# One step of a hybrid decoder on Trainium2: the up-projection's first block product in three passes, and another order for scale, operands and weight sums of the first pairs

## The chip, the cores and the metric

The kernel runs on one core of one Trainium2 chip. The metric is the device time of one execution in microseconds (us). Engines in the profile: PE (tensor engine, matmuls), PEld (its weight loads), DVE (vector engine), ACT (ScalarE), POOL (GpSimd), SP (the queue that issues most loads).

## What is computed

A one-layer decoder trunk is run on a prompt of 512 tokens and on 8 single-token samples, 520 columns in all. After the mixers the feed-forward part follows, on which the change works:

```python
x = x + jnp.matmul(mix, w_out)
y, conv_new = conv_ffn(rms_norm(x, norm2), w_up, conv_w, conv_b, w_down, conv_buf)

def conv_ffn(h, w_up, conv_w, conv_b, w_down, prefix):
    u = jnp.matmul(h, w_up)                       # 2048 -> 2 * 5632
    up = jnp.concatenate([prefix.astype(u.dtype), u], axis=1)
    c = conv_b
    for j in range(CONV_W):                       # causal depthwise convolution, width 3
        c = c + conv_w[j] * up[:, j:j + T]
    gate, val = jnp.split(c, 2, axis=-1)
    y = jnp.matmul(jax.nn.gelu(gate) * val, w_down)
```

Everything is float32, and the kernel must keep nearly that precision.

## The kernel before

**Products in three passes.** A float32 operand is split into hi (rounded to the reduced format fp32r, a ScalarE copy) and lo (the rest, a vector subtraction). A product is then hi x hi, hi x lo and lo x hi, three fp32r matmuls into one PSUM bank (lines 1139 to 1141, 967 and 186 to 190). A float32 matmul on unsplit operands (raw) is one instruction, which the profile shows as two records (lines 1146 and 1102).

**The up-projection in pairs.** The 88 column blocks of 128 are worked off in 44 pairs, p = 0 to 43, alternately gate and value. A pair is a 2 x 2 block product: its weights are A(p, n, i), with n the column block and i the half of the 2048 rows (even or odd blocks of 128), its operands B(i, t), with t the half of the 520 columns (260 each). From p = 1 on the pair needs seven block products instead of eight, by sums of weights and of operands. `up_units` has them as units numbered 1 to 7:

| unit | weights | operand | PSUM bank |
|---|---|---|---|
| 1 | A(p,0,0) | B11, raw | 1 |
| 2 | A(p,0,1) | B21 | 1, on top of 1 |
| 3 | S2 after `sum4` | B22 | 3, on top of 5 |
| 4 | A(p,1,1) | t4 | 4 |
| 5 | S1 | t1 | 3 |
| 6 | S2 | t2 | 2 |
| 7 | S3 | t3 | 0 |

The weight sums S1, S2 and S3 come from `sum1`, `sum2`, `sum3`, and S2 is overwritten by `sum4` (lines 1039 to 1048, vector engine, 128 x 1024 each, one buffer each). The operands t1 to t4 are sums and differences of the B(i, t); they are made once (`prep1` to `prep5`) and kept split. The results are put together by vector additions out of PSUM (`post6`, `c21`, `c22`, `post3`). Pair 0 does not use this scheme: `first_units` runs its eight products raw on xg, the activations that are not yet divided by their norm, and multiplies with that norm (rbc1) on the way out of PSUM (line 1108).

**Order of the work.** The order on each engine is that of the program. The loop at the end goes through the list of units: at unit k it first emits the split of unit k + 2 (`prod`: hi on ScalarE, lo on the vector engine, lines 929 and 931, three buffers each), then what is put ahead of unit k (`pre`: loads, weight sums, operands), then its matmuls, then `post`, then one step of each background generator. Each engine takes its instructions in this order and waits where an operand or a buffer is not ready.

**The convolution** of a finished pair (`conv`, lines 1050 to 1085) is such a generator. It begins with two small GpSimd copies and two ScalarE activations (line 1060) and goes on with four vector steps (line 1065), one per unit of the next pair. After a gate pair follows a ScalarE GELU, after a value pair a vector multiplication (line 1072) and a store.

**Loads.** `load_pair` loads the two blocks of a pair, 1 MB each, on the SP queue: block 0 into a buffer with two copies, block 1 into a single one (r2), so that the load of the next pair's block 1 waits for the lo of unit 4.

**Ahead of the up-projection** the output projection ends (line 967); `split_x2` makes for each pair of its blocks the scaled activations xg (`gain`, line 994), the squares (line 1005) and their sum (line 1007, GpSimd). `norm2` (called by `prep1`) sums the squares over the rows by matmuls with a constant (line 1223) and makes 1/rms (lines 1224 to 1226 on ScalarE, `newton` on the vector engine). `normed` multiplies xg by it (line 1233), `diff` subtracts (line 1247), `split_act` splits (lines 1241 and 1242). `prep0` stores the sums x2b to memory (GpSimd queue). Before the change these preparations hang on four units of pair 0 (one for each n and i, both halves t in it) and on two units of pair 1.

**After it** the down-projection (line 967) takes its operands back from memory (`load_a`, GpSimd queue, and `split_a`).

## Time and profile before

| | before |
|---|---|
| three runs, us | 2345.4, 2345.03, 2345.9 |
| median, us | 2345.4 |
| profiled execution, us | 2346.91 |
| its span on the core, us | 2345.0 |
| mean granted clock of the tensor engine | 0.993 |
| ScalarE busy, us | 863.0 (37%) |
| GpSimd busy, us | 185.1 (8%) |
| bytes moved | 268.68 MB, 115 GB/s |

In a row of a timeline stand the start in us from the span's start, the duration, the engine, the line of the kernel, the operation, what it writes and reads, and in brackets the idle time ahead of it with what ended that. In a row of waits stand who waited, for whom, the sum in us, how often, and the longest. In the chain of the work that ended last stand start, length and work; a number behind x counts the instructions in it. Pair 0 begins at 858.94 us of the span.

### The profile page before, as it was taken

The page shows a single profiled execution, that of the slowest core. Times are in us where ns is not written, and L with a number is a line of the kernel's source. Part 1 is how long each engine was busy: PE and PEld are TensorE (multiplying, and loading weights), DVE is VectorE, ACT ScalarE, POOL GpSimd, SP SyncE. Part 2 cuts the span into 40 slices and gives each one's busy share as a digit, 9 for nine tenths or more (in the row PEclk, how much of TensorE's full clock was granted, in tenths as well). Part 3 has the DMA queues.
Part 4 walks back from the last instruction along what each step waited for, and adds up shares of the span by engine and source line. Part 5 has one row for each costly group of instructions (what it writes and reads, how often), then busy time and mean ns, then how long its engine had stood idle before and what let it go on. Part 6 is the DMA issues. An engine that isn't in the chain of part 4 may idle for free.

```text
span 2345.0 us, 42285 instructions
## 1 busy us (share of the span) xinstructions
PE 2302.1 (98%) x18268; PEld 2260.4 (96%) x18268; DVE 1414.2 (60%) x1963; ACT 863.0 (37%) x1245; POOL 185.1 (8%) x397
## 2 busy tenths in 40 slices
PE   8999999999999997999999999999999999999996
PEld 8999999999999997999999999999999999999996
DVE  4365655445543448888878888788887433434346
ACT  6233342313342434444444444444444222222225
POOL 0001021021010120000000000000000000000002
PEclk9999999999999998999999999999999999999998
DMA  5322233334251443433334343343435523323214
GB/s 183 102 82 93 89 94 97 95 108 131 73 172 61 141 129 89 122 105 118 110 117 127 100 124 105 116 127 103 124 107 188 218 90 132 127 91 109 91 55 136
DMA packets 313353, 268.68 MB, mean 115 GB/s; under 512 B 8492, under 2 KB 299144, under 8 KB 311072
## 3 DMA queue, kind: packets, MB, share of 16 engines
q1 hardware_dynamic: 298608, 212.56, 29.5%
q0 software_dynamic: 14560, 53.43, 6.5%
q8 instruction: 144, 2.36, 0.4%
q14 instruction: 41, 0.34, 0.0%
HBM read 240.25 MB, written 28.12 MB: 114 GB/s over the span
## 4 chain that ended last, share of the span: by engine, by line
PE 73%; DVE 4%; ACT 1%; issue 1%; DMA 0%; ACTq 0%; DVEq 0%; POOLq 0%
PE pw L967 24%; PE pw L1139 10%; PE pw L1140 10%; PE pw L1141 10%; PE pw L1146 6%; PE pg L186 3%; PE pg L188 3%; PE pg L190 3%; DVE lo L931 1%; PE psc L703 1%; PE pob L685 1%; DVE n L1233 0%; PE pw L1102 0%; PE px L750 0%; ACT hi L929 0%
## 5 line engine op out<-in xcount | busy, mean ns | idle before, releaser
L929 ACT ACTIVATE hi<-r 128x1024 fp32r<-128x1024 f32 (+1 forms) x208 | 208.0, 1006 | 450.5 <-PE pw L967 364.8
L931 DVE TENSOR_TENSOR lo<-r,hi 128x1024 fp32r<-128x1024 f32 (+1 forms) x208 | 250.1, 1203 | 87.7 <-ACT hi L929 87.7
L186 PE MATMUL pg<-x1h,hi 128*128 128x260 f32 x1408 | 289.8, 287 | 3.1 <-ACT hi L157 1.8
L190 PE MATMUL pg<-x1h,lo 128*128 128x260 f32 x1408 | 284.5, 284 | 0.5 <-DVE lo L159 0.5
L188 PE MATMUL pg<-x1l,hi 128*128 128x260 f32 x1408 | 283.5, 283 | 0.0
L931 DVE TENSOR_TENSOR lo<-s,hi 128x1024 fp32r<-128x1024 f32 x172 | 210.4, 1223 | 65.3 <-ACT hi L929 65.3
L1326 DVE TENSOR_TENSOR x<-pw,x 128x260 f32<-128x260 f32 (+2 forms) x192 | 74.0, 423 | 268.3 <-PE pw L967 264.8
L159 DVE TENSOR_TENSOR lo<-raw,hi 128x1024 fp32r<-128x1024 f32 x104 | 127.2, 1223 | 168.0 <-ACT hi L157 156.4
L186 PEld LDWEIGHTS pg<-x1h,hi 128*128 128x128 f32 x1408 | 217.7, 189 | 4.4 <-ACT hi L157 2.0
L929 ACT ACTIVATE hi<-s 128x1024 fp32r<-128x1024 f32 x172 | 181.8, 1058 | 105.3 <-PE pw L1140 98.1
L190 PEld LDWEIGHTS pg<-x1h,lo 128*128 128x128 f32 x1408 | 217.5, 189 | 0.7 <-DVE lo L159 0.7
L188 PEld LDWEIGHTS pg<-x1l,hi 128*128 128x128 f32 x1408 | 217.2, 189 | 0.0
L1065 DVE SCALAR_TENSOR_TENSOR cv<-u,convc,cv 128x512 f32<-128x512 f32 (+1 forms) x176 | 132.2, 751 | 43.8 <-ACT cv L1060 43.8
L1146 PE MATMUL pw<-n,r 128*128 128x260 f32 x688 | 157.7, 382 | 0.0
L1146 PEld LDWEIGHTS pw<-n,r 128*128 128x128 f32 x688 | 127.6, 190 | 17.7
L157 ACT ACTIVATE hi<-raw 128x1024 fp32r<-128x1024 f32 x104 | 109.6, 1056 | 43.5 <-PE pg L188 36.6
L1139 PE MATMUL pw<-t4h,hi 128*128 128x260 f32 x344 | 106.3, 309 | 0.0
L1139 PE MATMUL pw<-t1h,hi 128*128 128x260 f32 x344 | 98.7, 287 | 6.7 <-DVE u L1108 6.7
L1060 ACT ACTIVATE cv<-u,convc 128x512 f32<-128x512 f32 x88 | 66.8, 806 | 99.3 <-DVE u L1185 93.8
L1141 PE MATMUL pw<-b21h,lo 128*128 128x260 f32 x344 | 98.2, 285 | 2.6 <-DVE lo L931 2.6
L1141 PE MATMUL pw<-t4h,lo 128*128 128x260 f32 x344 | 98.0, 285 | 2.3 <-DVE lo L931 2.3
L1139 PE MATMUL pw<-b22h,hi 128*128 128x260 f32 x344 | 97.6, 284 | 1.1 <-DVE u L1164 1.1
(475 smaller groups left out, 6173.4 us busy)
## 6 DMA issues: line engine op xcount, KB each, us to landing
r<-in_w_up SPq DMA_DIRECT2D x88, 1024.0 KB, 5.3
raw<-in_w_in SPq DMA_DIRECT2D x88, 512.0 KB, 3.6
r<-in_w_down SPq DMA_DIRECT2D x40, 1024.0 KB, 5.1
ad<-cv POOLq DMA_DIRECT2D x22, 520.0 KB, 3.1
a<-ad POOLq DMA_DIRECT2D x11, 1040.0 KB, 5.5
raw<-in_w_out SPq DMA_DIRECT2D x16, 512.0 KB, 3.4
r<-in_w_out SPq DMA_DIRECT2D x8, 1024.0 KB, 5.2
r<-in_w_down SPq DMA_DIRECT2D x13, 512.0 KB, 3.3
```

The lines of the kernel that those rows point to most:

```text
L159: V.tensor_tensor(lo, raw, hi.bitcast(F32), op=ALU.subtract)
L186: PE.matmul(ps[:, i, 0:b - a], wh, xh[:, a:b], start=first, stop=False)
L188: PE.matmul(ps[:, i, 0:b - a], wh, xl[:, a:b], start=False, stop=False)
L190: PE.matmul(ps[:, i, 0:b - a], wl, xh[:, a:b], start=False, stop=last)
L929: S.activation(hi, view, AF.Copy)
L931: V.tensor_tensor(lo, view, hi.bitcast(F32), op=ALU.subtract)
L967: PE.matmul(ps[t][:, 0:b - a], wt[:, kk], x[:, a:b], start=kk == 0 and wt is hi and x is xh, stop=kk == nk - 1 and wt is lo)
L1065: V.scalar_tensor_tensor(cv[:, j, 0:w], u[:, j, i:i + w], convc[:, i, n], cv[:, j, 0:w], op0=ALU.mult, op1=ALU.add)
L1139: PE.matmul(ps(k), hi[:, m], xh[:, m], start=a, stop=False, skip_group_check=True)
L1140: PE.matmul(ps(k), hi[:, m], xl[:, m], start=False, stop=False, skip_group_check=True)
L1141: PE.matmul(ps(k), lo[:, m], xh[:, m], start=False, stop=z, skip_group_check=True)
L1146: PE.matmul(ps(1), A(p, 0, 0)[:, m], xop["b11"][:, m], start=m == 0, stop=m == 7, skip_group_check=True)
```

## The change

Five things are done:

- From pair 3 on unit 1 is in three passes as well: its weights A(p,0,0) are split like the others, and B11 is split once (`prep_b11`, ahead of the sixth unit of pair 2; it borrows two buffers of the convolution). In pairs 1 and 2 unit 1 stays raw. In pair 1 units 2 and 3 become raw too.
- The order of the units from pair 2 on is 1, 4, 5, 6, 7, 2, 3 instead of 1, 4, 6, 7, 5, 2, 3. The result that needs unit 5 (`c22`) is now made right after unit 7, ahead of `c21`. Pair 1 keeps 1, 5, 6, 7, 2, 4, 3.
- Pair 0 has eight units of one raw product each instead of four of two. The norm and t1 hang on the second of them, t2 on the fifth, the weight sums S1 and S2 of pair 1 on the sixth; t3 and S3 on the first unit of pair 1, B21 and t4 on its third; the splits of B21 and B22 on the last unit of pair 1 and the first of pair 2.
- For the last two blocks of the output projection only one of four gains stands ahead of the squares, and the last sum of squares is the vector engine's.
- The down-projection's operands and the last output tiles use other buffers, and the first two of these operands are both loaded on the second unit of the last pair.

```diff
@@ -988,13 +988,14 @@
 
         m = n0 // 2
 
-        def gain():
-            for i in range(2):
-                for t in range(2):
-                    S.activation(xg[i][t][:, m], x2b[i][t][:, m], AF.Copy, scale=gv[:, G2 + n0 + i:G2 + n0 + i + 1])
-
-        if n0 == KT - 2:
-            gain()
+        end = n0 == KT - 2
+
+        def gain(some):
+            for i, t in some:
+                S.activation(xg[i][t][:, m], x2b[i][t][:, m], AF.Copy, scale=gv[:, G2 + n0 + i:G2 + n0 + i + 1])
+
+        if end:
+            gain([(0, 0)])
         if not sacc:
             sacc.append(by_halves(utile()[:, :, 0:TT]))
             sq = sacc[0]
@@ -1004,10 +1005,11 @@
             for t in range(2):
                 S.activation(sq[:, i, t], x2b[i][t][:, m], AF.Square)
         if n0:
-            G.tensor_tensor(sacc[0], sacc[0], sq, op=ALU.add)
-        yield
-        if n0 < KT - 2:
-            gain()
+            (V if end else G).tensor_tensor(sacc[0], sacc[0], sq, op=ALU.add)
+        if not end:
+            yield
+            gain([(0, 0)])
+        gain([(0, 1), (1, 0), (1, 1)])
 
     def wout_evac(n, t, a, b, ps):
         xt = x2b[n % 2][t][:, n // 2]
@@ -1020,7 +1022,7 @@
 
 
 
-    xop = {}
+    xop, B = {}, {}
     R, SS, GT, UC = {}, {}, {}, {}
     pairs = [(c, o, part) for c in range(NCH) for o in (0, 2) for part in range(2)]
 
@@ -1092,25 +1094,24 @@
 
         bank, uu = {}, []
 
-        def unit(i, n):
+        def unit(i, n, t):
             def mm(un):
-                for t in range(2):
-                    if i == 0:
-                        bank[n, t] = bankp(2 - 2 * n + t)
-                    ps = bank[n, t][:, 0:HALF]
-                    for m in range(8):
-                        PE.matmul(ps, A(0, n, i)[:, m], xg[i][t][:, m], start=i == 0 and m == 0,
-                                  stop=i == 1 and m == 7, skip_group_check=True)
-                    if i == 1:
-                        if not uu:
-                            uu.append(utile())
-                            G.memset(uu[0][:, :, 0:2], 0.0)
-                        V.tensor_tensor(uu[0][:, n, 2 + HALF * t:2 + HALF * (t + 1)], ps,
-                                        rbc1[:, HALF * t:HALF * (t + 1)], op=ALU.mult)
-
-            return Unit(None, mm, (lambda: start_conv(0, uu[0])) if (i, n) == (1, 0) else None)
-
-        return [unit(i, n) for n in (1, 0) for i in range(2)]
+                if i == 0:
+                    bank[n, t] = bankp(2 - 2 * n + t)
+                ps = bank[n, t][:, 0:HALF]
+                for m in range(8):
+                    PE.matmul(ps, A(0, n, i)[:, m], xg[i][t][:, m], start=i == 0 and m == 0,
+                              stop=i == 1 and m == 7, skip_group_check=True)
+                if i == 1:
+                    if not uu:
+                        uu.append(utile())
+                        G.memset(uu[0][:, :, 0:2], 0.0)
+                    V.tensor_tensor(uu[0][:, n, 2 + HALF * t:2 + HALF * (t + 1)], ps,
+                                    rbc1[:, HALF * t:HALF * (t + 1)], op=ALU.mult)
+
+            return Unit(None, mm, (lambda: start_conv(0, uu[0])) if (i, n, t) == (1, 0, 1) else None)
+
+        return [unit(i, n, t) for n in (1, 0) for i in range(2) for t in range(2)]
 
     def up_units(p):
         first = p == 1
@@ -1141,10 +1142,12 @@
                     PE.matmul(ps(k), lo[:, m], xh[:, m], start=False, stop=z, skip_group_check=True)
             return mm
 
-        def mm_raw(un):
-            for m in range(8):
-                PE.matmul(ps(1), A(p, 0, 0)[:, m], xop["b11"][:, m], start=m == 0, stop=m == 7,
-                          skip_group_check=True)
+        def mm_raw(k, w, x, fresh):
+            def mm(un):
+                for m in range(8):
+                    PE.matmul(ps(k), w()[:, m], B[x][:, m], start=fresh and m == 0, stop=m == 7,
+                              skip_group_check=True)
+            return mm
 
         def add(name, a, k):
             st[name] = fwork([P, HALF], name)
@@ -1165,14 +1168,9 @@
 
         def post7():
             add("q3", "q2", 0)
-            if first:
-                c22()
-            else:
+            c22()
+            if not first:
                 c21()
-
-        def post5():
-            if not first:
-                c22()
 
         def post2():
             S.copy(out(0, 0), ps(1))
@@ -1186,22 +1184,30 @@
             start_conv(p, u())
 
         nx = p + 1 if p + 1 < len(pairs) else None
-        U = {1: Unit(None, mm_raw, post1),
-             4: Unit(lambda: split(A(p, 1, 1)), mm_split(4, "t4", True), post4),
+        U = {4: Unit(lambda: split(A(p, 1, 1)), mm_split(4, "t4", True), post4),
+             5: Unit(lambda: split(SS[p, 1]), mm_split(3, "t1", True)),
              6: Unit(lambda: split(SS[p, 2]), mm_split(2, "t2", True), post6),
-             7: Unit(lambda: split(SS[p, 3]), mm_split(0, "t3", True), post7),
-             5: Unit(lambda: split(SS[p, 1]), mm_split(3, "t1", True), post5),
-             2: Unit(lambda: split(A(p, 0, 1)), mm_split(1, "b21", False), post2),
-             3: Unit(lambda: split(SS[p, 2]), mm_split(3, "b22", False), post3)}
-        seq = (1, 5, 6, 7, 2, 4, 3) if first else (1, 4, 6, 7, 5, 2, 3)
+             7: Unit(lambda: split(SS[p, 3]), mm_split(0, "t3", True), post7)}
+        if p < 3:
+            U[1] = Unit(None, mm_raw(1, lambda: A(p, 0, 0), (1, 1), True), post1)
+        else:
+            U[1] = Unit(lambda: split(A(p, 0, 0)), mm_split(1, "b11", True), post1)
+        if first:
+            U[2] = Unit(None, mm_raw(1, lambda: A(p, 0, 1), (2, 1), False), post2)
+            U[3] = Unit(None, mm_raw(3, lambda: SS[p, 2], (2, 2), False), post3)
+        else:
+            U[2] = Unit(lambda: split(A(p, 0, 1)), mm_split(1, "b21", False), post2)
+            U[3] = Unit(lambda: split(SS[p, 2]), mm_split(3, "b22", False), post3)
+        seq = (1, 5, 6, 7, 2, 4, 3) if first else (1, 4, 5, 6, 7, 2, 3)
         at = [U[n] for n in seq]
         at[3 if first else 2].pre.append(lambda: sum4(p))
+        if p == 2:
+            at[0].pre.append(lambda: sum2(p))
         if nx is not None:
             at[0].pre.append(lambda: load_pair(nx, 0))
             if first:
                 at[4].pre.append(lambda: load_pair(nx, 1))
-                at[5].pre.append(lambda: (sum1(nx), sum3(nx)))
-                at[6].pre.append(lambda: sum2(nx))
+                at[6].pre.append(lambda: (sum1(nx), sum3(nx)))
             else:
                 at[0].pre.append(lambda: load_pair(nx, 1))
                 at[3].pre.append(lambda: sum1(nx))
@@ -1246,8 +1252,6 @@
         for k in (0, 4):
             V.tensor_tensor(out[:, k:k + 4], a[:, k:k + 4], b[:, k:k + 4], op=ALU.subtract)
 
-    B = {}
-
     def prep0():
         drain()
         for i in range(2):
@@ -1255,40 +1259,57 @@
                 nc.gpsimd.dma_start(x2d.rearrange("p (m i) c -> p i m c", i=2)[:, i, :, HALF * t:HALF * (t + 1)],
                                     x2b[i][t])
 
-    def prep1():
+    def prep_t1():
         norm2()
         B[1, 2] = normed(0, 1, 12)
-        B[1, 1] = xop["b11"] = normed(0, 0, 13)
+        B[1, 1] = normed(0, 0, 13)
         B["t"] = slot(0, "t12", F32)
         diff(B["t"], B[1, 2], B[1, 1])
         xop["t1"] = split_act(B["t"], 1, 2, "t1")
 
-    def prep2():
+    def prep_t2():
         B[2, 2] = normed(1, 1, 3)
         diff(B["t"], B[2, 2], B["t"])
         xop["t2"] = split_act(B["t"], 4, 5, "t2")
+
+    def prep_t3():
         diff(B[1, 2], B[2, 2], B[1, 2])
         xop["t3"] = split_act(B[1, 2], 6, 7, "t3")
 
-    def prep3():
-        sum1(1)
-        sum3(1)
-        sum2(1)
-
-    def prep4():
+    def prep_t4():
+        diff(B["t"], B["t"], B[2, 1])
+        xop["t4"] = split_act(B["t"], 9, 12, "t4")
+
+    def prep_b11():
+
+        hi = slot(3, "b11h")
+        S.activation(hi, B[1, 1], AF.Copy)
+        halves = []
+        for a in (0, 4):
+            h = ff.tile([P, 4, HALF], F32R, tag="cv", name="b11x", bufs=3)
+            V.tensor_tensor(h, B[1, 1][:, a:a + 4], hi[:, a:a + 4].bitcast(F32), op=ALU.subtract)
+            halves.append(h)
+        lo = slot(13, "b11l")
+        for a, h in zip((0, 4), halves):
+            S.activation(lo[:, a:a + 4], h.bitcast(F32), AF.Copy)
+        xop["b11"] = hi, lo
+
+    def split_b(i, t, name, h, l):
+        xop[name] = split_act(B[i, t], h, l, name)
+
+    def prep_n21():
         B[2, 1] = normed(1, 0, 8)
-        diff(B["t"], B["t"], B[2, 1])
-        xop["b21"] = split_act(B[2, 1], 10, 11, "b21")
-
-    def prep5():
-        xop["t4"] = split_act(B["t"], 9, 12, "t4")
-        xop["b22"] = split_act(B[2, 2], 8, 0, "b22")
-
-    ups[0][0].pre += [prep0, lambda: load_pair(1, 0)]
-    ups[0][1].pre.append(prep1)
-    ups[0][2].pre += [lambda: load_pair(1, 1), prep2, prep3]
-    ups[1][1].pre.append(prep4)
-    ups[1][2].pre.append(prep5)
+
+    N, U1, U2 = ups[:3]
+    N[0].pre += [prep0, lambda: load_pair(1, 0)]
+    N[1].pre.append(prep_t1)
+    N[4].pre += [lambda: load_pair(1, 1), prep_t2]
+    N[5].pre += [lambda: sum1(1), lambda: sum2(1)]
+    U1[0].pre += [prep_t3, lambda: sum3(1)]
+    U1[2].pre += [prep_n21, prep_t4]
+    U1[6].pre.append(lambda: split_b(2, 1, "b21", 10, 11))
+    U2[0].pre.append(lambda: split_b(2, 2, "b22", 8, 0))
+    U2[5].pre.append(prep_b11)
 
     wo_units[10].pre.append(lambda: load_pair(0, 0))
     wo_units[12].pre.append(lambda: load_pair(0, 1))
@@ -1296,7 +1317,7 @@
 
     x2 = [None] * 4
     a_raw, a_hl = {}, {}
-    SETS = (((9, 12), (4, 5)), ((6, 7), (1, 2)))
+    SETS = (((9, 12), (1, 2)), ((4, 5), (6, 7)))
 
     def load_a(c):
         a_raw[c] = bigt((3, 13)[c % 2], f"a{c}", F32)
@@ -1353,8 +1374,8 @@
     for g in range(ngroup - 1):
         down_units[16 * g].pre.append(lambda g=g: bg.append(next_a(g + 1)))
     last = ups[-1]
-    last[0].pre += [lambda: load_a(0), lambda: load_d(0), lambda: load_d(1)]
-    last[1].pre.append(lambda: load_a(1))
+    last[0].pre += [lambda: load_d(0), lambda: load_d(1)]
+    last[1].pre += [lambda: load_a(0), lambda: load_a(1)]
     last[4].pre += [lambda: split_a(0), lambda: load_d(2)]
     last[5].pre.append(lambda: split_a(1))
     down_units[0].pre += [lambda: load_x2(0), lambda: load_x2(1)]
@@ -1366,7 +1387,7 @@
     def tail_start():
         drain()
         ln_exp_tables()
-        ys.extend(bigt(s, f"y{t}", F32).rearrange("p k t -> p (k t)") for t, s in enumerate((9, 12, 4, 5)))
+        ys.extend(bigt(s, f"y{t}", F32).rearrange("p k t -> p (k t)") for t, s in enumerate((9, 12, 1, 2)))
         sums[-1] = fwork([P, NB, KT], "q1")
 
     down_units[2 * ntail].pre.append(tail_start)
```

## Prediction

> **What bounds the kernel now.** I read the busy shares first, then the windows by stage, then the chain of work that ended last, then the engines' timelines inside one pair of the up-projection, and last those of its first three pairs.
>
> ```profile
> PE 2302.1 (98%) x18268; PEld 2260.4 (96%) x18268; DVE 1414.2 (60%) x1963; ACT 863.0 (37%) x1245; POOL 185.1 (8%) x397
> ```
>
> ```profile
> core 0 of [0], span 2345.0 us
> ...
> 866.00:951.31 85.31, 71.59 (x426) 66.08 (x425) 73.58 (x77) 33.93 (x39) 2.88 (x10) 0.92 0.43 128
> 951.31:1806.55 855.24, 855.24 (x6572) 835.55 (x6572) 691.02 (x801) 371.45 (x446) 50.36 (x185) 1.00 0.39 117
> ```
>
> In the windows the columns after the length are PE, PEld, DVE, ACT and POOL busy, the granted clock, and the DMA share. From 951.31 to 1806.55 the tensor engine is never idle at a clock of 1.00: whatever shortens its stream there shortens the kernel. From 866 to 951 it is different: PE is idle 13.7 us and granted 0.92, while the vector engine is busy 73.58 of 85.31 us. The first stage is the vector engine's, the second the tensor engine's, and the change touches both.
>
> ```profile
> 951.31 3.51 PE pw L1146 x16
> 972.12 3.51 PE pw L1146 x16
> ...
> 1785.75 3.51 PE pw L1146 x16
> 1806.55 28.84 PE pw L967 x240
> ```
>
> The chain gives the price list. Each L1146 line is the first block product of one pair, taken raw: 16 records in 3.51 us. From pair 4's (972.12) to the end of pair 43 (1806.55) 40 pairs pass, so a pair takes 834.43 / 40 = 20.86 us. The other six products, 24 matmuls each, take (20.86 - 3.51) / 6 = 2.89 us each. The L967 line gives the same: 28.84 / 240 x 24 = 2.88 us.
>
> **The tensor engine's gain from pair 3 on.** The changed product runs the same 24 matmuls as its six neighbours, on operands of the same shape: 3.51 - 2.89 = 0.62 us less for each of pairs 3 to 43. The added weight loads are those of any 24-matmul unit, so they are in the 2.89. For the 40 pairs from pair 4 on this is 24.8 us. Pair 3 is counted with the first stage.
>
> The page "TensorE: Matmul & The Clock Gate" of the Trainium skill (Back-to-back issue gap) gives an isolated matmul N/2.4 + 2.5 ns, so an estimate of 110.8 ns for 260 columns, and by that price 24 would take 2.66 us and the gain would be 0.85 us a pair. The trace has 120 ns (28.84 / 240) in this very stream, so the trace decides, and the sum goes on with 2.89.
>
> **What the gain needs from the other engines.** A product in three passes needs one more split in each pair: a ScalarE copy (hi) and a vector subtraction (lo). The vector engine takes its work in order, and this is how it looks around a pair's border:
>
> ```profile
> 1152.79 1.24 DVE L1072 TENSOR_TENSOR cv<-cv 128x1040 f32<-128x1040 f32 x1
> 1153.94 1.22 DVE L931 TENSOR_TENSOR lo<-s,hi 128x1024 fp32r<-128x1024 f32 x1
> 1155.08 1.22 DVE L1042 TENSOR_TENSOR s<-r,r 128x1024 f32<-128x1024 f32 x1
> 1156.22 0.42 DVE L1164 TENSOR_TENSOR u<-q,pw 128x260 f32<-128x260 f32 x1
> 1156.55 1.22 DVE L1045 TENSOR_TENSOR s<-s,r 128x1024 f32<-128x1024 f32 x1
> ...
> 1159.95 0.43 DVE L1185 TENSOR_TENSOR u<-q,pw 128x260 f32<-128x260 f32 x1 [0.28 <-PE pw L1141]
> 1161.67 0.75 DVE L1065 SCALAR_TENSOR_TENSOR cv<-u,convc,cv 128x512 f32<-128x512 f32 x1 [1.30 <-ACT cv L1060]
> 1163.32 1.23 DVE L931 TENSOR_TENSOR lo<-s,hi 128x1024 fp32r<-128x1024 f32 x1 [0.90 <-ACT hi L929]
> 1164.46 0.75 DVE L1065 SCALAR_TENSOR_TENSOR cv<-u,convc,cv 128x520 f32<-128x520 f32 x1
> 1165.13 1.22 DVE L931 TENSOR_TENSOR lo<-s,hi 128x1024 fp32r<-128x1024 f32 x1
> ```
>
> Start to start, where nothing is waited for, a lo or a weight sum takes 1.14 us, a convolution step 0.67, an addition from PSUM 0.34, the gate multiplication of every second pair 1.15. A pair then holds 7 lo, 4 sums, 4 steps and 5 additions: 12.54 + 2.68 + 1.70 = 16.9 us, and 18.1 with the multiplication. Two waits come back in each pair, since the convolution's start goes through ScalarE before the next hi: 1.30 and 0.90 us. That makes 19.1 us and 20.3 us, on average 19.7, against a new period of 20.86 - 0.62 = 20.24. The heavy pair fits to within 0.1 us, and the light one gives back 1.1.
>
> I then laid the new order (1, 4, 5, 6, 7, 2, 3) out against units of 2.89 us, time zero at the pair's start, heavy pair. The lo of the third unit ends at 4.5 and is needed at 5.8; of the fourth 6.2 against 8.7; of the fifth 8.2 against 11.6; of the sixth 11.2 against 14.5; of the seventh 15.0 against 17.3; the new one, for the next pair's first unit, 18.3 against 20.2. The seventh unit adds onto the bank that holds the third unit's result, so its start (17.3) waits for the addition that reads that bank; this now stands right behind the fifth unit's own addition and ends at 16.8. So the tightest margins are 0.5 us there and 1.3 us at the third unit. I cost the steady stage at no stall. What hides the new split is 0.5 us of vector slack a pair; without that cover, each 0.1 us a pair costs 4 us.
>
> The hi copies are held back by their buffers:
>
> ```profile
> ACT hi L929 <- PE pw L1140: 170.4, 102, 1.9
> DVE lo L931 <- ACT hi L929: 109.5, 123, 1.8
> ```
>
> Three hi buffers now serve seven splits a pair instead of six, so each copy, without exception, starts when the unit before has let its buffer go. It then has two units, 5.8 us, before its own. ScalarE has the room (371.45 of 855.24 us busy).
>
> **The first three pairs.**
>
> ```profile
> 858.94 7.17 PE L1102 MATMUL pw<-xg,r 128*128 128x260 f32 x32
> 865.95 1.92 PE L1223 MATMUL ms<-u,onesD 128*128 128x260 f32 x8
> ```
>
> ```profile
> 860.31 1.33 ACT L1005 ACTIVATE cv<-x 128x260 f32<-128x260 f32 x4
> ```
>
> ```profile
> 861.78 2.21 POOL L1007 TENSOR_TENSOR u<-u,cv 128x1040 f32<-128x1040 f32 x1 [10.69 <-ACT cv L1005]
> ```
>
> ```profile
> 869.83 0.70 DVE L214 TENSOR_TENSOR cv<-rbc 128x520 f32<-128x520 f32 x1 [10.04 <-ACT rbc L1226]
> ```
>
> The norm's matmuls (865.95) stand behind two raw products in the queue; the sum they read is ready at 863.99. The new units hold one product each, so they can go 3.51 us earlier, at 862.6. The sum must be there by then: two of the four squares no longer wait for the last tile, three of the four gains stand behind them, and the last addition is the vector engine's (1.24) instead of GpSimd's (2.21). I put it at 861.5. The vector chain of the norm then begins at 866.3 instead of 869.8. GpSimd, free of that sum, issues the four stores of x2b earlier; they only give room to the weight load behind them.
>
> From there the vector engine is the bound, and I walked its new order with the steps above (1.15 for the 1040-wide ones). First unit of pair 1 at 889.0, raw; the second (now t1) has its lo at 889.3 and runs without a wait, where it began at 899.12 before. Its fourth waits 3.2 us for the weight sum that stands behind t3; the sixth 1.7 us. Pair 1's two other raw products cost 2 x 0.62 more, and save two splits. Their end is at 917.7. Pair 2's second weight load waits for the lo that frees its buffer, and that now ends at 911.5:
>
> ```profile
> 920.28 6.02 DMA r<-in_w_up
> ```
>
> So it lands at 917.5 instead of 926.3. Pair 2 then waits 4.3 us at its third unit (the lo stands behind the split of B21 and pair 1's convolution), 0.7 and 1.9 us later on, and ends at 947.1. The first unit of pair 3 needs B11 split, two vector halves at 946.7 to 949.1, a ScalarE copy behind them, and the copy that frees its bank: it starts at 950.6, against 951.31 before. The early start is nearly all spent, since the vector engine has as much to do as before: two lo fewer, one lo and two halves more.
>
> Such waits have a second price:
>
> ```profile
> 899.12 0.56 PE L1139 MATMUL pw<-t1h,hi 128*128 128x260 f32 x1 [6.70 <-DVE u L1108]
> ...
> 913.36 0.39 PE L1141 MATMUL pw<-b21h,lo 128*128 128x260 f32 x1 [2.56 <-DVE lo L931]
> ...
> 914.45 0.42 PE L1140 MATMUL pw<-b21l,hi 128*128 128x260 f32 x1
> ...
> 917.26 0.42 PE L1141 MATMUL pw<-b21h,lo 128*128 128x260 f32 x1
> ```
>
> After an idle 2.56 us the matmuls ran about 3.4 us at half speed (0.42 instead of 0.28), which costs 1.7 us where PE is the bound. Pair 3 begins after 3.5 us of idling, so I add 1.7 there: pair 4 would start at 972.5, against 972.12. The skill's same page (What's actually happening) has the clock halved only after an idle window of about 3.4 us; by its letter the shorter waits would cost nothing. The trace shows 2.56 us to be enough.
>
> Bounds of this part: with none of the vector waits in my walk (9.7 us in sum) pair 3 starts 9.6 us earlier than before; with an error of the same kind the other way, 5 us later.
>
> The end: the first two down-projection operands are now fetched behind the last pair's first unit.
>
> ```profile
> a<-ad POOLq DMA_DIRECT2D x11, 1040.0 KB, 5.5
> ```
>
> Issued at 2.9 and landing by about 9 us in that pair, the first is split from 11.6 on: no cost, but 3 us if that cover were gone. The buffer names exchanged for the down-projection and the last tiles change no time.
>
> **Sum.** -24.8 from pairs 4 to 43, +0.4 from all before: -24.4 us on the span of 2345.0. The profiled execution took 2346.91 and the three runs have a median of 2345.4, so I take the difference off the median: 2321.0 us.
>
> **The rivals.**
> 1. Forecast: the steady stage without stall, the front even. 2321, its own range 2316 to 2327. Chance 0.66.
> 2. The vector engine is late in the heavy pairs. It decides once a pair needs on average 0.5 us more than I laid out. For it: the margin of 0.1 us in those pairs. Against it: the light pairs recover. A further 0.25 to 0.5 us a pair gives back 10 to 20 us: 2331 to 2341. Chance 0.19, of which 0.04 within no change.
> 3. Slower: the vector engine becomes the bound with all its waits kept. It is busy 691.02 / 41 = 16.85 us a pair and waits 4.0. With one lo more and the same 4.0 the period is 22.0, 1.14 x 41 = 47 us over before: 2392. It decides when the waits stay above 2.9 us. Against it: most of the 109.5 us waits for hi, and that for PE to let a buffer go, so it shrinks once the vector engine is late. Chance 0.05.
> 4. The new matmuls run at half a raw record, 3.51 / 16 / 2 = 0.110 us: 2.63 us a product, 36 us gained, 2310. The stream at 0.120 next to it speaks against it. This is what the page's formula would give. Chance 0.02.
> 5. The front loses its vector waits: 2312. Chance 0.08.
>
> **The numbers.** The range 2314 to 2333 takes in the forecast, half of rival 5 and the near part of rival 2, some 0.8 together. About 0.2% is what a measurement can tell from no change here. Faster by more: 0.66 + 0.15 + 0.02 + 0.08 = 0.91; same 0.04; slower 0.05.
>
> **What would show it.** Right: pairs 20.2 us apart on the chain with no L1146 piece after pair 2, PE without idle from pair 4 on, vector busy near 18 us a pair, the norm's matmuls near 862.6, t1 in pair 1 without a wait, pair 3 starting near 950. Wrong: PE waiting for a lo or for the addition ahead of the seventh unit in every second pair (rival 2) or in each (rival 3); a matmul spacing other than 0.120.

## The result and the profile after

The changed kernel took 2320.03 us (median of 4 runs, 2319.45 to 2320.68) against 2345.64 us (2345.03 to 2345.9, 4 runs) before: a ratio of 0.9891, with a 95% interval of 0.9874 to 0.9908. The profiled execution took 2320.68 us, with a span of 2318.9 us.

The busy shares of the page, engine by engine, as before: us, share of the span, instructions.

```profile
PE 2277.2 (98%) x18580; PEld 2254.3 (97%) x18580; DVE 1458.5 (63%) x2005; ACT 903.3 (39%) x1287; POOL 184.4 (8%) x396
```

The tensor engine's busy time fell by 24.9 us (2302.1 to 2277.2), and the vector engine's rose by 44.3 us (1414.2 to 1458.5). The added vector work is larger than the gain, so where it lies decides. The windows of the changed kernel show that; their columns are those of the windows before.

```profile
core 0 of [0], span 2318.9 us
...
866.00:950.43 84.43, 71.41 (x407) 64.75 (x405) 73.47 (x77) 33.98 (x37) 1.38 (x7) 0.93 0.29 89
...
950.43:972.83 22.40, 22.40 (x169) 22.40 (x170) 18.60 (x21) 11.37 (x13) 0.37 (x3) 0.90 0.33 95
...
972.83:1781.49 808.66, 808.66 (x6734) 808.66 (x6733) 714.69 (x820) 397.96 (x474) 51.51 (x182) 1.00 0.40 121
```

The last row holds pairs 4 to 43. The tensor engine is busy for all of it at a clock of 1.00, and a pair takes 808.66 / 40 = 20.217 us, where it took 834.43 / 40 = 20.861. That is 25.8 us for the 40 pairs. The vector engine works 714.69 / 40 = 17.87 of each 20.22 us. The row above is pair 3 alone: 22.40 us at a clock of 0.90, 2.2 us more than a later pair.

The chain of waits, in order of time (start, us, what), shows how the first stage ends. Pair 0 is the L1103 piece, the norm's matmuls are L1229.

```profile
858.55 3.51 PE pw L1103 x16
862.06 1.77 PE ms L1229 x8
...
910.95 5.33 DMA r<-in_w_up
...
948.09 2.03 ACT b11l L1294 x2
950.12 0.27 ACT u L1176
950.43 0.58 PE pw L1140
...
1781.49 28.79 PE pw L967 x240
1810.38 443.31 PE pw L967 x3696
```

From the first matmul of pair 0 (by the chain, whose pieces begin 0.16 us behind the timeline's in both kernels) to the end of pair 43 the span was 1806.55 - 859.10 = 947.45 us, and is 1781.49 - 858.55 = 922.94 us: 24.5 us less. Of that, the way to pair 4 takes 114.28 us instead of 113.02 (+1.3), and the 40 pairs give 25.8. I call this stretch the stage below. The rest of the span's 26.1 us lies outside this stage: pair 0 starts 0.55 us earlier, and what follows pair 43, where the change exchanges buffers and no work, takes 537.4 instead of 538.45 us. Both vary by about a microsecond between profiles: pair 0 starts at 858.55 in this one and at 859.83 in another of the same kernel, and the tail takes from 537.4 to 538.6 us in the runs below that are built on the changed kernel. The profile before is also of an execution of 2346.91 us, 1.3 above its median. So the stage is the sharper measure of single profiles.

The tensor engine's timeline of the changed kernel in its first pairs shows the waits behind each idle stretch, in brackets.

```profile
888.19 3.67 PE L1148 MATMUL pw<-n,r 128*128 128x260 f32 x16
899.93 0.39 PE L1140 MATMUL pw<-t3h,hi 128*128 128x260 f32 x1 [2.28 <-ACT hi L929]
901.19 0.59 PE L1142 MATMUL pw<-t3h,lo 128*128 128x260 f32 x1 [0.75 <-DVE lo L931]
...
917.24 3.67 PE L1148 MATMUL pw<-n,r 128*128 128x260 f32 x16
926.22 0.39 PE L1140 MATMUL pw<-t1h,hi 128*128 128x260 f32 x1 [2.43 <-ACT hi L929]
927.48 0.39 PE L1142 MATMUL pw<-t1h,lo 128*128 128x260 f32 x1 [0.75 <-DVE lo L931]
932.73 0.39 PE L1142 MATMUL pw<-t2h,lo 128*128 128x260 f32 x1 [0.57 <-DVE lo L931]
943.24 0.36 PE L1140 MATMUL pw<-b22h,hi 128*128 128x260 f32 x1 [1.83 <-DVE u L1167]
950.43 0.58 PE L1140 MATMUL pw<-b11h,hi 128*128 128x260 f32 x1 [4.06 <-ACT u L1176]
```

No t1 matmul of pair 1 stands there with a wait, and the longest idle stretch, 4.06 us, is the one before pair 3, whose first operand is B11's split. What ends it is the copy that frees pair 3's bank (L1176); on ScalarE it stands behind the two copies of B11's split, which end at 950.12 on the chain.

### The profile page after: what moved, and what is told of

Read it like the earlier page. It is cut to its first block, busy times and chain, and to the rows that moved or that the text cites. A ratio compares the mean times of both kernels' runs of the same rounds, so it can differ in the third digit from the quotient of the medians.

```text
span 2318.9 us, 43111 instructions
## 1 busy us (share of the span) xinstructions
PE 2277.2 (98%) x18580; PEld 2254.3 (97%) x18580; DVE 1458.5 (63%) x2005; ACT 903.3 (39%) x1287; POOL 184.4 (8%) x396
## 4 chain that ended last, share of the span: by engine, by line
PE 72%; DVE 3%; ACT 1%; issue 1%; DMA 0%; ACTq 0%; DVEq 0%; POOLq 0%
PE pw L967 25%; PE pw L1142 12%; PE pw L1141 12%; PE pw L1140 12%; PE pg L186 3%; PE pg L190 3%; PE pg L188 3%; DVE lo L931 1%; PE psc L703 1%; PE pob L685 1%; DVE n L1239 0%; ACT hi L929 0%; PE px L750 0%; DVE x L1347 0%; PE ppt L693 0%
## 5 line engine op out<-in xcount | busy, mean ns | idle before, releaser
L929 ACT ACTIVATE hi<-r 128x1024 fp32r<-128x1024 f32 (+1 forms) x248 | 250.7, 1015 | 504.6 <-PE pw L967 363.4
L931 DVE TENSOR_TENSOR lo<-r,hi 128x1024 fp32r<-128x1024 f32 (+1 forms) x248 | 298.6, 1205 | 54.2 <-ACT hi L929 54.2
L1140 PE MATMUL pw<-t3h,hi 128*128 128x260 f32 x344 | 98.5, 286 | 2.3 <-ACT hi L929 2.3
L1142 PE MATMUL pw<-t3h,lo 128*128 128x260 f32 x344 | 98.4, 286 | 0.8 <-DVE lo L931 0.8
L1142 PE MATMUL pw<-t1h,lo 128*128 128x260 f32 x344 | 98.0, 285 | 0.8 <-DVE lo L931 0.8
L1140 PE MATMUL pw<-t4h,hi 128*128 128x260 f32 x344 | 97.9, 285 | 0.0
L1141 PE MATMUL pw<-t3l,hi 128*128 128x260 f32 x344 | 97.9, 285 | 0.0
L1142 PE MATMUL pw<-t2h,lo 128*128 128x260 f32 x344 | 97.3, 283 | 0.6 <-DVE lo L931 0.6
```

Of the source, the lines that this page charges most:

```text
L929: S.activation(hi, view, AF.Copy)
L931: V.tensor_tensor(lo, view, hi.bitcast(F32), op=ALU.subtract)
L1140: PE.matmul(ps(k), hi[:, m], xh[:, m], start=a, stop=False, skip_group_check=True)
L1141: PE.matmul(ps(k), hi[:, m], xl[:, m], start=False, stop=False, skip_group_check=True)
L1142: PE.matmul(ps(k), lo[:, m], xh[:, m], start=False, stop=z, skip_group_check=True)
```

## The experiments

Every edit is made on the changed kernel, except where the text names the kernel before. The stage is each profile's own. The kernel before, run beside each group on the same chip, had medians of 2345.96, 2345.69 and 2345.6 us.

**One part alone: the preparation.** All pairs keep the raw first product, and B11 is never split.

```
-        if p < 3:
+        if p < len(pairs):
...
-    U2[5].pre.append(prep_b11)
```

> The changed kernel with the first product raw in every pair again, and without the split of B11; order of units and preparation stay changed. Theory (the gain is the tensor engine's, 0.645 us for each of 40 pairs, and the new preparation is worth little): pairs 20.86 us apart again, which costs 25.8 us; pair 3 starts some 3 us earlier and without the slow stretch, since the two vector halves of B11 and the ScalarE copy are gone, which saves about 4.9 us. 2320.0 + 25.8 - 4.9 = 2340.9 us. Rival A (the preparation alone is worth nothing): 2345.6. Rival B (the new order of the units or the preparation carries most of the gain): below 2335.

Measured: 2341.11 us (2339.94 to 2341.42), ratio 0.9979 (0.997 to 0.9988); the stage took 1800.68 - 858.96 = 941.72 us. Pair 4 starts at 967.62 on its chain, 108.66 us after pair 0. So the preparation of the first pairs is worth 4.4 us up to pair 4. Another 1.4 us come after it: (1800.68 - 967.62) / 40 = 20.83 us a pair, where the kernel before has 20.86. The lengths of single pairs show where they lie. Pairs 4, 5 and 6 take 20.91, 20.81 and 20.90 us in the kernel before (starts on its chain at 972.12, 993.03, 1013.84 and 1034.74), and 20.92, 20.80 and 20.79 in this run, which has the new order of the units as well (967.62, 988.54, 1009.34, 1030.13). The kernel before loses 0.1 us in pair 6, and in every fourth after it, ahead of the seventh unit:

```profile
1031.07 0.42 DVE L1164 TENSOR_TENSOR u<-q,pw 128x260 f32<-128x260 f32 x1
...
1031.63 0.36 PE L1139 MATMUL pw<-b22h,hi 128*128 128x260 f32 x1
...
1031.83 0.28 PE L1140 MATMUL pw<-b22l,hi 128*128 128x260 f32 x1
```

The unit starts 0.14 us behind the end of the addition (1031.49) that reads its bank, and its second matmul follows after 0.20 us, where 0.12 is usual. The new order makes that addition earlier, and the wait is gone; it is about 1 of the 1.4 us. Pair 4 keeps its 0.12 us, as does every fourth pair of all these kernels: it holds one matmul more, a transposition for the convolution (line 1077 before, 1079 after). Busy shares show nothing of such a wait, since the records of neighbouring matmuls overlap.

The changed kernel beside this run shows what B11's split costs at the start, with the slow stretch behind its wait and less what three passes save in pair 3: 114.28 - 108.66 = 5.6 us. Three passes bring 833.06 - 808.66 = 24.4 us from pair 4 on.

**One part alone: three passes.** The kernel before, with its own first pairs and its own order of units, takes the first product in three passes from pair 3 on.

```
-        U = {1: Unit(None, mm_raw, post1),
+        U = {1: Unit(None, mm_raw, post1) if p < 3 else
+             Unit(lambda: split(A(p, 0, 0)), mm_split(1, "b11", True), post1),
...
+    ups[2][5].pre.append(prep_b11)
...
+    last[1].pre += [lambda: load_a(0), lambda: load_a(1)]
```

> The kernel before with the three passes of the first product from pair 3 on alone (and the split of B11 on the sixth unit of pair 2); old order of units, old preparation. Theory: pairs 20.22 us apart, 25.8 us gained; the vector halves, the split and the copies behind them put pair 3 at about 954 instead of 951.3, and the idling costs one slow stretch of 1.7 us, 3.9 us lost in all: 2345.6 - 25.8 + 3.9 = 2323.7 us. Rival (the new order is what makes room for the seventh split): PE waits in every second pair or in each, 2331 or more.

Measured: 2327.78 us (2327.3 to 2329.42), ratio 0.9924 (0.9911 to 0.9938); stage 927.52 us. Pair 4 started at 976.14, as expected. The tensor engine shows next to no idle time in the 40 pairs, in the old order too. So the rival, that the new order of units first makes the room, falls with its 2331 us. But the small wait of the old order is back: pairs 4 to 7 take 20.30, 20.20, 20.29 and 20.19 us, where the changed kernel has 20.30, 20.18, 20.18 and 20.18. By the windows row of this kernel the new order is worth 0.04 us a pair (810.32 / 40 = 20.258 instead of 20.217).

```profile
976.14:1786.46 810.32, 810.19 (x6734) 809.63 (x6733) 714.53 (x821) 397.89 (x474) 49.83 (x182) 1.00 0.40 121
```

The expected time was 4 us too low. 1.6 us are this; about 0.6 lie in the way to pair 4 and in the tail after pair 43 (538.7 us instead of the 538.45 before). The remaining 1.8 us come of setting medians beside profiles: the profiled execution before took 1.3 us more than its median, and the one here 0.5 us less.

**The old order of units in the changed kernel.**

```
-        seq = (1, 5, 6, 7, 2, 4, 3) if first else (1, 4, 5, 6, 7, 2, 3)
+        seq = (1, 5, 6, 7, 2, 4, 3) if first else (1, 4, 6, 7, 5, 2, 3)
...
-            if p == 2:
-                at[0].pre.append(lambda: sum2(p))
...
-                at[6].pre.append(lambda: (sum1(nx), sum3(nx)))
+                at[6].pre.append(lambda: (sum1(nx), sum3(nx), sum2(nx)))
```

(c22 moves back behind unit 5 with it.)

> The changed kernel with the old order of units 1, 4, 6, 7, 5, 2, 3 from pair 2 on; the result that needs the fifth product is made after that product again. Theory: the order changes no wait of the tensor engine in the steady stage, 2320 within 2 us. Rival: the new order makes the room for the seventh split, then pairs are more than 20.3 us apart and the time is above 2324.

Measured: 2322.93 us (2322.47 to 2324.06), ratio 0.9902 (0.9888 to 0.9915); stage 923.9 us. Pair 4 starts at 972.68, so a pair takes (1782.78 - 972.68) / 40 = 20.253 us, and pairs 4 to 7 take 20.31, 20.19, 20.29 and 20.20: the small wait again. The order is worth 1.4 us in the 40 pairs, 1 us by the stage and up to 3 by the medians (which for one and the same kernel can differ by 1.9 us from group to group, see the later splits below), a small part of the 25.6.

**B11's two subtractions on GpSimd.**

```
-            V.tensor_tensor(h, B[1, 1][:, a:a + 4], hi[:, a:a + 4].bitcast(F32), op=ALU.subtract)
+            G.tensor_tensor(h, B[1, 1][:, a:a + 4], hi[:, a:a + 4].bitcast(F32), op=ALU.subtract)
```

(The two halves become plain float32 tiles, and the copies behind them read them as such.)

> The changed kernel with the two subtractions of the split of B11 on GpSimd instead of the vector engine. Theory (the wait of 4.1 us ahead of pair 3 stands in the vector engine's order): at about 2.2 us each GpSimd has them by 946, the ScalarE copies are done by 947, pair 3 starts near 947 instead of 950.4 without a long idle and without a slow stretch: about 5 us less, 2315. Rival A (the wait is ScalarE's chain or the copy that frees the bank): no change, 2320. Rival B (GpSimd and the vector engine slow each other): 2320 or more.

Measured: 2321.8 us (2320.22 to 2322.41), ratio 0.9895 (0.9882 to 0.9909); stage 922.3 us. The expected 5 us did not come. The timeline of this kernel shows why:

```profile
941.35 1.22 DVE L1044 TENSOR_TENSOR s<-r,r 128x1024 f32<-128x1024 f32 x1
...
942.10 6.07 POOL L1290 TENSOR_TENSOR b11x<-n,b11h 128x1040 f32<-128x1040 f32 x2 [0.58 <-ACT b11h L1286]
...
943.62 2.31 DVE L931 TENSOR_TENSOR lo<-r,hi 128x1024 fp32r<-128x1024 f32 x1
945.85 3.41 DVE L1047 TENSOR_TENSOR s<-s,r 128x1024 f32<-128x1024 f32 x1
...
948.21 2.03 ACT L1294 ACTIVATE b11l<-b11x 128x1040 fp32r<-128x1040 f32 x2 [6.19 <-POOL b11x L1290]
...
950.14 0.35 ACT L1176 COPY u<-pw 128x260 f32<-128x260 f32 x1
...
950.55 0.39 PE L1140 MATMUL pw<-b11h,hi 128*128 128x260 f32 x1 [3.92 <-ACT u L1176]
```

The two vector instructions that lie beside GpSimd's take 2.31 and 3.41 us instead of 1.22, and GpSimd's take 2.73 and 3.37, where one took 2.21 in the kernel before. The rows read as turns. GpSimd's first, whose record begins at 942.10, ends at 944.83, 2.26 us behind the sum that ran before it (941.35 + 1.22 = 942.57); the lo ends 1.10 us after that, at 945.93; GpSimd's second 2.24 us after that, at 948.17; the second sum 1.09 us after that, at 949.26. Each of the four takes about its own length once the one before it is done. The Trainium skill, page "SBUF — State Buffer" (Who interferes with whom), says that a vector instruction with two SBUF inputs and a GpSimd instruction that reads SBUF hold each other up, the later one waiting until the earlier has ended; these rows agree. Pair 3 starts at 950.55, as without the move (950.43). Rival A, a wait of ScalarE's own, has no room here: ScalarE's copies start 0.04 us behind GpSimd's end, and the copy that frees the bank follows them.

**The vector engine's slack in the steady stage, by a small load.** The addition behind unit 6 is made twice from pair 4 on.

```
             add("q2", "q1", 2)
+            if p > 3:
+                V.tensor_tensor(st["q2"], st["q1"], ps(2), op=ALU.add)
```

> The changed kernel with one small vector instruction more in each pair from pair 4 on: the addition of the fourth unit's product out of PSUM is done twice (same result), 0.34 us. In the changed kernel's trace the vector engine is idle 94.0 us in 40 pairs, 2.35 a pair, of which 1.92 are the two waits for ScalarE at the pair's start: 0.43 us a pair are left. Theory (that slack covers the new split): 0.34 fits, no change within 1 us, 2320. Rival (the vector engine is already what the tensor engine waits for in the heavy pairs): 0.34 x 40 = 13.6 us more, or half of that if only every second pair pays: 2327 to 2334.

Measured: 2325.0 us (2324.09 to 2325.35), ratio 0.9911 (0.9897 to 0.9924), and (1785.43 - 973.07) / 40 = 20.309 us a pair. That is between the two expectations, because the loss is not spread over the pairs: the starts of pairs 4 to 7 lie at 973.07, 993.49, 1013.67 and 1034.08, so pairs with the gate multiplication (4 and 6) take 20.42 and 20.41 us and the one between takes 20.18. The timeline around the start of the seventh unit in pair 6, first in the changed kernel:

```profile
1029.72 0.42 DVE L1167 TENSOR_TENSOR u<-q,pw 128x260 f32<-128x260 f32 x1
...
1030.59 0.28 PE L1140 MATMUL pw<-b22h,hi 128*128 128x260 f32 x1
```

and with the doubled addition, where the code stands two lines lower:

```profile
1030.57 0.42 DVE L1169 TENSOR_TENSOR u<-q,pw 128x260 f32<-128x260 f32 x1
...
1031.14 0.36 PE L1140 MATMUL pw<-b22h,hi 128*128 128x260 f32 x1
```

The unit waits for that addition. In the changed kernel 1030.59 - 1029.72 - 0.42 = 0.45 us lie between, and in the loaded kernel 0.15, which is the hand-over itself. So the true slack of a heavy pair is about 0.3 us. The second addition holds the queue up by more than the 0.34 us expected: the two start at 1025.90 and 1026.36 and the gate multiplication behind them at 1026.70, 0.80 us behind the first addition instead of 0.34, so 0.46 us are added. The 0.16 us beyond the slack, and the second matmul of the unit, which follows after 0.20 us instead of 0.12, are the 0.24 us that a heavy pair loses (20.42 against 20.18). Idle time does not show them: the tensor engine counts as busy for 812.28 of the 812.36 us.

**A larger load.** sum1 of the next pair is made twice in pairs 4 to 42.

```
+                if p > 3:
+                    at[3].pre.append(lambda: V.tensor_tensor(SS[nx, 1], A(nx, 1, 0), A(nx, 1, 1), op=ALU.add))
```

> The changed kernel with one large vector instruction more in pairs 4 to 42: the weight sum of the sixth unit's place is made twice (same result), 1.14 us. Theory (0.43 us of slack a pair, then the vector engine sets the pace): (1.14 - 0.43) x 39 = 28 us more, 2348, with PE waiting for lo in each pair and pairs 20.9 us apart. Rival A (the two waits for ScalarE shrink once the vector engine is late, so that the slack is really 2.35): no change, 2320. Rival B (no slack at all): 44 us more, 2364.

Measured: 2348.44 us (2347.33 to 2349.75), ratio 1.0011 (1.0002 to 1.002): 1.14 us of vector work a pair take all the gain away. The mean is the expected one, (1807.97 - 973.28) / 40 = 20.87 us a pair, and again it falls on the heavy pairs: pairs 4 and 6 take 21.21 and 21.40 us, pair 5 takes 20.27 (starts at 973.28, 994.49, 1014.76 and 1036.16). The waits of the tensor engine from 1000 to 1770 in this kernel (us in total, times, longest) are not the expected one for a lo in each pair, but one for the addition in every second pair, so the expected time came by another path:

```profile
PE pw L1140 <- DVE u L1167: 17.1, 18, 1.1
```

**Three splits moved away from the start.** The first product stays raw in pairs 3 and 4, B22's product in pair 2 too, and the splits of B21, B22 and B11 go to later units.

```
-        if p < 3:
+        if p < 5:
             U[1] = Unit(None, mm_raw(1, lambda: A(p, 0, 0), (1, 1), True), post1)
...
+        if p < 3:
+            U[3] = Unit(None, mm_raw(3, lambda: SS[p, 2], (2, 2), False), post3)
...
-    U1[6].pre.append(lambda: split_b(2, 1, "b21", 10, 11))
-    U2[0].pre.append(lambda: split_b(2, 2, "b22", 8, 0))
-    U2[5].pre.append(prep_b11)
+    U1[5].pre.append(lambda: split_b(2, 1, "b21", 10, 11))
+    U2[5].pre.append(lambda: split_b(2, 2, "b22", 8, 0))
+    ups[4][4].pre.append(prep_b11)
```

> The changed kernel with vector work taken out of its first pairs: the first product stays raw up to pair 4 and the third unit's up to pair 2, B21 is split on the sixth unit of pair 1, B22 on the sixth of pair 2, B11 on the fifth of pair 4. Nothing is left out. Theory (in the first pairs the vector engine is the bound, and a raw product costs PE 0.63 us but saves the vector engine 1.14 and puts a split off): laid out with the durations of the traces, pair 9 starts 6 us earlier, 2314. Rival (the first pairs are bound by something else, the weight loads or ScalarE): the three raw products more cost 1.9 us, 2322.

Measured: 2318.99 us (2318.09 to 2319.52), ratio 0.9887 (0.9871 to 0.9902); stage 1778.73 - 859.78 = 918.95 us, 4.0 less than the changed kernel's. The expected 6 us did not come in full. The median was only 1.0 below the changed kernel's, which came from another group of runs, so the two were put side by side:

> The changed kernel itself, beside the two versions with less vector work in the first pairs: 2320.

> The version with the later splits again, on the same chip as the changed kernel. Theory (the vector engine bounds the first pairs; between the starts of pairs 0 and 5 its first run was 4.3 us shorter than the changed kernel, 130.4 against 134.7 us): 3 to 4 us less than the changed kernel beside it. Rival (the gain does not come through to the end): within 1 us of it.

Measured: the changed kernel 2320.96 us (2320.03 to 2322.16), ratio 0.9893 (0.9877 to 0.991); with the later splits 2317.11 us (2316.53 to 2317.84), ratio 0.9878 (0.9864 to 0.9893). That is 3.85 us less, and no run of one lies among the runs of the other. The windows of the stage, first the changed kernel's in this group, then with the later splits:

```profile
859.83:1782.91 923.08, 908.68 (x7340) 901.19 (x7340) 809.01 (x921) 447.46 (x532) 55.06 (x195) 0.99 0.39 119
```

```profile
858.79:1777.66 918.87, 909.38 (x7316) 899.28 (x7316) 805.18 (x918) 443.58 (x529) 55.03 (x195) 1.00 0.39 120
```

The stage gives 4.2 us: idle time of the tensor engine falls from 14.4 to 9.5 us (length less PE busy). The clock after the wait differs as well. Two equal windows of the span, which do not hold the same matmuls (granted clock in the third column from the end), in the changed kernel's first profile and then with the later splits:

```profile
950.50:953.90 3.40, 3.40 (x16) 3.40 (x17) 1.56 (x2) 1.63 (x3) 0.37 (x3) 0.50 0.03 6
953.90:957.30 3.40, 3.40 (x25) 3.40 (x25) 2.45 (x3) 3.00 (x5) 0.00 (x0) 0.82 1.01 300
```

```profile
950.50:953.90 3.40, 2.96 (x24) 2.96 (x25) 3.40 (x5) 1.45 (x3) 0.00 (x0) 1.00 0.29 85
953.90:957.30 3.40, 3.40 (x31) 3.40 (x30) 3.40 (x4) 1.81 (x2) 0.00 (x0) 1.00 0.00 0
```

The changed kernel comes out of its 4.06 us wait at a clock of 0.50 and 0.82. With the later splits that wait is gone, and the clock is 1.00 here. This kernel beats the one before and the changed one. Three splits are moved and three more products are raw at once, so the run does not say what B11's split alone brings.

**On top of that, sum3 of pair 1 earlier.** It moves from pair 1's first unit into the last unit of pair 0.

```
-    N[5].pre += [lambda: sum1(1), lambda: sum2(1)]
-    U1[0].pre += [prep_t3, lambda: sum3(1)]
+    N[5].pre += [lambda: sum1(1), lambda: sum2(1), lambda: sum3(1)]
+    U1[0].pre.append(prep_t3)
```

> As the version with the later splits, and the weight sum S3 of pair 1 is made with S1 and S2 on the sixth unit of pair 0, not behind t3. Theory (the wait ahead of the fourth unit of pair 1, 2.3 us there, stands in the row S3, hi, lo behind t3): about 0.6 us less than the version without it by the layout, 2 us if the slow stretch behind that wait goes too: 2317 to 2318.5. Rival (the vector engine has the same work either way, and the wait only moves): no change, 2319.

Measured: 2318.37 us (2316.81 to 2319.28), ratio 0.9883 (0.9868 to 0.9898), and a stage of 918.48 us against 918.87 without it. That is no gain: the wait at t3 falls from 2.29 to 1.14 us, the next one rises from 0.46 to 1.36, and the one ahead of t4's third matmul from 0.68 to 1.62.

**The norm's chain later.** The preparation of t1 is queued one unit later.

```
-    N[1].pre.append(prep_t1)
+    N[2].pre.append(prep_t1)
```

> The changed kernel with the norm and t1 hung on the third unit of pair 0 instead of the second, so that the norm's matmuls stand behind two raw products in the queue as in the kernel before. Theory (the vector chain sets the first pairs, so a later start of it comes through in full): 3.5 us more, 2323.8. Rival (the start of the chain is hidden): 2320.

Measured: 2324.8 us (2323.77 to 2325.92), ratio 0.9911 (0.9897 to 0.9924). The stage takes 926.73 us, 3.8 more than the changed kernel's 922.94; pair 4 starts at 977.67. The norm's matmuls start 7.01 instead of 3.51 us behind pair 0's first, and those 3.5 us come through in full. So in the first pairs it is the chain behind the norm, most of it vector work, that sets the time.

## Why the prediction was right

The forecast of 2321.0 us came from -24.8 for pairs 4 to 43 and +0.4 for all before, -24.4 in sum. The stage measured -24.5, from -25.8 and +1.3: two small misses that cancel. The medians lie 25.6 apart; the last microsecond is that of the start and end outside the stage, which the runs do not explain further.

**The tensor engine's gain.** 0.62 us a pair was predicted, 0.645 measured. By the run with the preparation alone, the passes bring (833.06 - 808.66) / 40 = 0.61. The other 1.4 us in 40 pairs come with the new order of the units (the run with the old order has the same 1.4), most of them by the 0.1 us wait ahead of the seventh unit of every fourth pair, which it takes away; the working had no term for it. The price of 0.120 us a matmul held (443.31 / 3696 = 0.1199, and 20.18 / 168 = 0.1201 in a pair), so rival 4 with 0.110 is out, and with it the prediction's estimate of 110.8 ns from the Trainium skill's page "TensorE: Matmul & The Clock Gate" (Back-to-back issue gap).

**The vector engine's slack.** Nothing waits in pairs 4 to 43, as costed: they take 20.18 us each, and every fourth, with the transposition, 20.31. The margin at the seventh unit was put at 0.5 us where the timeline has 0.45. What the working left out is that 0.15 of it is the hand-over from the addition to the matmul. The prediction gave rival 2 a chance of 0.19, and the loads show how near it was: 0.46 us more in the vector queue of a pair start it, in the heavy pairs alone, and 1.14 us use the whole gain up. The statement that light pairs recover holds only for the vector engine: the tensor engine, which is in order and has no slack, does not win back what a heavy pair loses. Rival 3, with all old waits kept, did not come. The new waits show it for 950.43 to 1781.5 in the changed kernel:

```profile
ACT hi L929 <- PE pw L1141: 229.6, 152, 1.9
DVE lo L931 <- ACT hi L929: 47.8, 64, 3.4
...
DVE cv L1067 <- ACT cv L1062: 41.0, 41, 1.2
```

The vector engine's waits for hi fell from 109.5 us to 47.8, while it had more to do: they were slack of the engine that waits, not a need.

**The first pairs.** The walk was near at each mark: the norm's matmuls 862.1 (862.6 predicted), pair 1 at 888.2 (889.0), pair 2 at 917.2 (917.7), pair 3 at 950.43 (950.6), its wait 4.06 us (3.5). The waits that the walk names ahead of pair 3 add up to 11.8 us, not to the 9.7 of its bound; measured were 9.0 (13.02 us idle from 866.00 to 950.43, less the 4.06). The term that was mis-sized is the slow stretch after that wait, 1.7 us in the sum and 2.2 measured: the matmuls lay 0.22 us apart until 955.3, for 4.9 us and not 3.4. Pair 4 started 0.7 us later than before (972.83 against 972.12) instead of 0.4; the +1.3 counts from pair 0, which began 0.55 us earlier. Rival 5, the loss of the vector waits, did not come in the changed kernel; with three splits moved, 4 us of it did.

**The shorter waits.** The prediction set the trace against the clock rule of the Trainium skill's page "TensorE: Matmul & The Clock Gate" (What's actually happening), by whose letter only an idle window of about 3.4 us halves the clock. Windows of the changed kernel around the wait of 2.28 us that ends at 899.93:

```profile
896.00:899.60 3.60, 1.65 (x14) 1.43 (x12) 3.46 (x4) 1.42 (x3) 0.00 (x0) 1.00 0.00 0
900.00:903.40 3.40, 2.65 (x12) 2.44 (x13) 3.40 (x4) 0.00 (x0) 0.00 (x0) 0.57 0.00 0
903.40:906.80 3.40, 3.40 (x16) 3.30 (x16) 3.40 (x4) 1.43 (x2) 0.00 (x0) 0.50 0.02 5
```

The clock is 1.00 before and 0.57 and 0.50 behind it. In this profile a second wait lies between: the two matmuls behind the first still ran at full pace (0.39 and 0.28 us), and those behind the wait of 0.75 us are slow (0.59, then 0.42). With the later splits a wait of 2.29 us was enough alone, since the first matmul behind it is already slow:

```profile
900.18 0.59 PE L1140 MATMUL pw<-t3h,hi 128*128 128x260 f32 x1 [2.29 <-ACT hi L929]
900.56 0.42 PE L1141 MATMUL pw<-t3l,hi 128*128 128x260 f32 x1
```

So the trace decides against the letter: an idle stretch of 2.3 us can be enough. After the wait of 1.83 us at 943.24 the clock stayed at 1.00; where the border lies, the runs do not show.

**The parts costed at nothing.** The tail's first piece takes 28.79 us (28.84 before), so the down-projection operands, fetched later, cost nothing.

## What to carry to other kernels

Read an engine's slack at the heaviest period, against the one matmul that waits for it, and take the hand-over off: an average over pairs hid here that 0.3 us were left. Compare the lengths of single periods, too: a busy share of 100% hid waits of 0.1 us in every fourth pair of the old order. Where a change adds work to a second engine, load that engine with a known extra and see where the period gives way; two such runs turn a margin that was argued into one that is measured. An operand that is needed only for cheaper passes can be prepared later, at the price of a few dear ones (0.6 us each here), while the engine that prepares it is the bound.

## What the runs showed of the hardware

Work moved from the vector engine to GpSimd did not run beside the vector engine's own: the two took turns, and both grew, from 1.22 to 2.31 and 3.41 us and from 2.21 to 2.73 and 3.37 us, as long as both read two tiles from SBUF. Vector additions with one operand out of PSUM kept their 0.42 us beside GpSimd's first. To move two such subtractions is therefore no way to unload the vector engine here.

A wait of 0.1 to 0.2 us ahead of a matmul does not show as idle time of the tensor engine; the lengths of the pairs show it. The clock's loss after short waits stood in the trace before already (2.56 us). With the later splits the wait of 4.06 us and the slow stretch behind it are gone. What the clock has of the 4.2 us is not measured apart; as an estimate, the three raw products more cost 3 x 0.62 = 1.9 us, the tensor engine's busy time rose by only 0.7, and so about 1.2 us are the clock's.
